# Hybrid decoder trunk on one core: the rotary stage's loads move to GpSimd's queue, the constants are made sooner, raw weights get a third buffer

## The chip, the core and the metric

The kernel runs on one core of a Trainium2 chip. The metric is the device time of one launch in microseconds (us), and lower is better. A core has TensorE (PE, matrix products), VectorE (DVE), ScalarE (ACT), GpSimd (POOL) and SyncE (SP). SP computes nothing here: it issues DMA transfers. ACT and POOL issue DMAs too, between their other instructions. Each engine works through its own list of instructions in order, so an instruction that waits holds up all that stand behind it on the same engine.

## What is computed

The reference is a two-layer decoder trunk on a sequence of 1024 tokens with 1024 channels. Each layer normalizes, projects once to 5376 columns, runs two token mixers side by side and merges them through gates:

```python
for layer in range(DEPTH):
    h = rms_norm(x, norm_w[layer])
    proj = h @ w_in[layer]
    (q, k, v, z_attn, q_h, f_h, i_h, g_h, gate_attn, gate_hgrn) = jnp.split(proj, split_points, axis=-1)
    q = partial_rope(q.reshape(B, T, N_HEADS, HEAD_DIM), positions)
    k = partial_rope(k.reshape(B, T, N_KV_HEADS, HEAD_DIM), positions)
    a = sliding_window_attention(q, k, v, attn_sinks[layer]) * jax.nn.silu(z_attn)
    ...
    b = o.reshape(B, T, HGRN_WIDTH) * jax.nn.silu(g_h)
    merged = (jax.nn.sigmoid(gate_attn) * (a @ w_up_attn[layer])
              + jax.nn.sigmoid(gate_hgrn) * (b @ w_up_hgrn[layer]))
    x = x + merged @ w_out[layer]
return rms_norm(x, final_norm_w)
```

`partial_rope` turns only the first 16 of each head's 64 channels: it multiplies by a cosine, and adds the partner channel (8 away) times a sine. Everything is float32.

## The kernel before

**Stages of a layer.** Normalize and transpose the activations, split every float32 number into a high and a low part (three matrix products then stand for one). Then 15 *pairs* (`pair`, L273): each takes two chunks of 128 columns of `w_in`, with a scheme that needs seven block products instead of eight; a block product is a group of 12 matmuls of 128x512. Where the first of the seven has been made ahead (`pair_first`, `gate_first`; the first 12 pairs of layer 0 and the first 11 of layer 1, L35), a pair is five groups, 60 matmuls, else seven. Then attention (L700 to L812), the recurrence (`core`, L866), the up-projections and the output projection.

**A pair's weights.** `load_chunk` (L85) loads a raw chunk of 512 KB into a tile with the tag `wraw` of the pool `wp`, which has two buffers (L48); SP issues it. A pair has two chunks, `wr` 0 and 1. DVE forms sums of their halves (L282, L283, L285, L286), ACT and DVE split those (L130, L131, L290, L291). The last reader of chunk 0 is L286 (where the first product was made ahead), of chunk 1 it is L291; only then is their buffer free for a later chunk.

**Results.** Two PSUM tiles `pb` and `pc` take a pair's groups in turn (three buffers, `pj`), DVE adds them out (L307), ACT applies scale or gate (`result`, L523) and stores to DRAM: `yd` for q, k and v, `gd` and `zd` for gates.

**Rotary.** `rotary` (L601) is a generator that the pairs from `TURN` = 9 on step forward once for each result (`use`, L641). It loads two tables, `cosT` and `sinT`, from DRAM (L604), and then for each of five tiles of q and k: the tile `y` (L610) and, with four small loads of 8 partitions each, the partner channels into the one tile `other` (L615), which stays in use from tile to tile. DVE multiplies by the tables and adds (L617, L619, L620), ACT and DVE split (L623, L625), and GpSimd stores the parts to `ksd` and `qsd` (L629 to L634), from where attention loads them (L689, L691). All loads of `rotary` are issued by SP.

**Constants.** `constants` (L393) is another generator, stepped once behind each pair (L646). Its last four steps make the tables: GpSimd clears a tile `tab` (L479), DVE fills it (L482 to L487), TensorE transposes it (L490), ACT copies and stores it (L492, L493).

**Memory.** Nearly all other big tiles are *slots* of 4 KB per partition in one pool of `NSLOT` = 40 that go round in turn, so a tile waits until the last reader of the tile that had its slot before is done.

**What sets the order.** The kernel is written as one sequence; a scheduler orders the instructions of each engine by what they need and when it expects that, and puts in the waits. The order that it makes is fixed when the kernel is built.

Of the kernel before, what the change touches and what calls it, by code (L numbers as in the profile page):

```python
# [10 lines left out]
F32 = mybir.dt.float32  # L11
# [6 lines left out]
P = 128  # L18
# [10 lines left out]
HALF = 8  # L29
IN_W = 5376  # L30
OQ, OKV, OZ, OQH, OF, OI, OG, OGA, OGH = 0, 512, 768, 1280, 1792, 2304, 2816, 3328, 4352
NLEV = 7
NSLOT = 40
NPAIR = 15
AHEAD = (12, 11)  # L35
TURN = 9
# [4 lines left out]
def trunk_kernel(ctx, tc, x, positions, norm_w, w_in, attn_sinks, hgrn_norm_w, w_up_attn,  # L41
                 w_up_hgrn, w_out, lb_logits, final_norm_w, c_ident, c_side, c_upper, c_diag, c_lev,
                 c_freq, out):
    nc = tc.nc
# [3 lines left out]
    wp = ctx.enter_context(tc.tile_pool(name="wp", bufs=2))  # L48
    sp = ctx.enter_context(tc.tile_pool(name="sp", bufs=NSLOT))
    ap_ = ctx.enter_context(tc.tile_pool(name="ap", bufs=2))  # L50
# [6 lines left out]
    def slot(shape, name, dt=F32):  # L57
        return sp.tile(shape, dt, tag="slot", name=name)
# [24 lines left out]
        return xn  # L83

    def load_chunk(w, c0, nm, k=KT, wide=False):  # L85
        raw = slot([P, k, P], f"wr_{nm}") if wide else wp.tile([P, k, P], F32, tag="wraw", name=f"wr_{nm}")
        nc.sync.dma_start(raw, w[:, c0:c0 + P].rearrange("(k p) c -> p k c", p=P))
        return raw

# [44 lines left out]
    def chunk(w, c0, nm, k=KT):  # L134

        return split_w(load_chunk(w, c0, nm, k), nm, [P, k, P])
# [238 lines left out]
    def split_rows(w, c0, n, nm, first=0):  # L375


        g = 1024 // n
        res = {}
        for k in range(0, KT, g):  # L380
            raw = wp.tile([P, g, n], F32, tag="wraw", name=f"wr_{nm}_{k}")
            nc.sync.dma_start(raw, w[k * P:(k + g) * P, c0:c0 + n].rearrange("(k p) c -> p k c", p=P))
            hi, lo = (split_w if k < first else split_slot)(raw, f"{nm}_{k}", [P, g, n])
            for j in range(g):
                res[k + j] = (hi[:, j], lo[:, j])
        return res


    tabs = [dp.tile([P, T], F32, name=f"tabs_{i}") for i in range(2)]
# [115 lines left out]
    consts = constants()  # L505


    for L in range(DEPTH):
# [5 lines left out]
        yd = [dp.tile([P, T], F32, name=f"yd_{L}_{j}") for j in range(6)]  # L514
# [8 lines left out]
        def result(m, c, r, o, src, own=None):  # L523

            n = src.shape[1]
            eng = nc.gpsimd if L == 0 and len(p1s) < 6 else nc.scalar
            d = own if own is not None else hp.tile([P, n], F32, tag="po", name=f"pq_{L}_{m}_{c}_{o}")
            if m < 3:
                S.activation(d, src, AF.Copy, scale=qkv[r][1])
                eng.dma_start(yd[r][:, o:o + n], d)  # L530
            elif m < 11 or c >= OG:
                S.activation(d, src, AF.Sigmoid if r < 2 * KT else AF.Silu)  # L532
                eng.dma_start(gd[r * P:(r + 1) * P, o:o + n], d)
            else:
                S.activation(d, src, AF.Silu)
                eng.dma_start(zd[:, r, o:o + n], d)
# [63 lines left out]

        def rotary():  # L601
            cosT, sinT = (slot([P, T], f"{n}T_{L}") for n in ("cos", "sin"))
            for t, d in zip((cosT, sinT), tabs):
                nc.sync.dma_start(t, d)  # L604

            o = slot([P, T], f"other_{L}")
            G.memset(o, 0.0)
            for n, j in enumerate((0, 1, 2, 4, 5)):
                y = slot([P, T], f"y_{L}_{j}")
                nc.sync.dma_start(y, yd[j])  # L610
                for r in range(2):
                    for i in range(2):
                        a = r * HD + i * HALF
                        b = r * HD + (1 - i) * HALF
                        nc.sync.dma_start(o[a:a + HALF], yd[j][b:b + HALF])  # L615
                yield
                V.tensor_tensor(out=y, in0=y, in1=cosT, op=ALU.mult)  # L617
                yield
                V.tensor_tensor(out=o, in0=o, in1=sinT, op=ALU.mult)  # L619
                V.tensor_tensor(out=y, in0=y, in1=o, op=ALU.add)  # L620
                yield
                hi = slot([P, T], f"yh_{L}_{j}", F32R)
                S.copy(hi, y)  # L623
                lo = y.bitcast(F32R)
                V.tensor_tensor(out=lo, in0=y, in1=hi.bitcast(F32), op=ALU.subtract)  # L625
                if n == 0:
                    for g, (own, far) in enumerate(((LO, HI), (HI, LO))):
                        for d, u in ((ksd[g][1 - g], (hi, lo)), (ksd[g][g], (lo, hi))):
                            nc.gpsimd.dma_start(d[own], u[0][own].bitcast(F32))  # L629
                            nc.gpsimd.dma_start(d[far], u[1][own].bitcast(F32))  # L630
                else:
                    for d, own, far in ((qsd[n - 1][0], LO, HI), (qsd[n - 1][1], HI, LO)):
                        nc.gpsimd.dma_start(d[own], hi[own].bitcast(F32))
                        nc.gpsimd.dma_start(d[far], lo[own].bitcast(F32))  # L634
                yield

        turning = rotary()
        for m in range(NPAIR):
            (c0, r0), (c1, r1) = pairs[m]

            def use(j, a, src, own):  # L641
                result(m, *pairs[m][j], a * 512, src, src if own else None)
                if m >= TURN:
                    next(turning, None)
            pair(wi, (c0, c1), parts, hT, f"{L}_{m}", p1s[m] if m < ahead else None, use)
            next(consts, None)  # L646
            if m == NPAIR - 2:
                vT, vn = slot([P, T], f"vT_{L}"), [slot([P, NB, P], f"vn_{L}")]
                nc.sync.dma_start(vT, yd[3])
# [35 lines left out]
        V.tensor_tensor(out=vd, in0=vn[0][:, 1:], in1=vn[0][:, :NB - 1], op=ALU.subtract)  # L685
        ks, qs = [], []
        wis = split_rows(wi, OI, 512, f"i{L}", 4)
        for g in range(2):
            ks.append([back(ksd[g][r], f"ks_{L}_{g}_{r}", nc.gpsimd) for r in range(2)])  # L689
# [125 lines left out]


        def up_load(w, m, nm):
            raw = wp.tile([P, 4, 2 * P], F32, tag="wraw", name=f"wr_{nm}")
            nc.sync.dma_start(raw, w[:, m * P:(m + 2) * P].rearrange("(k p) c -> p k c", p=P))
            return raw  # L820

        def up_chunk(w, m, nm):
            return split_w(up_load(w, m, nm), nm, [P, 4, 2 * P])
# [293 lines left out]

        wo = {}
        raws = [up_load(w_up_hgrn[L], 0, f"uh{L}_0")]
        for m in range(0, KT, 2):  # L1120
            w = split_w(raws.pop(0), f"uh{L}_{m}", [P, 4, 2 * P])
# [4 lines left out]
            for a in range(2):  # L1126
                u, t = u2s[m // 2][a]
# [19 lines left out]
        def split_a(a, nm):  # L1147
            return [split_slot(t, f"m{L}_{nm}_{i}", [P, 2, 512]) for i, t in enumerate(a)]
# [62 lines left out]
        m = split_a(a11, "s2")  # L1211
# [4 lines left out]
        m = split_a(a21, "s1")  # L1216
# [8 lines left out]
        m = split_a(a12, "s4")  # L1225
# [4 lines left out]
        m = split_a(a11, "s3")  # L1230
# [63 lines left out]
```

## Time and profile before

| what | value |
|---|---|
| time, median of 3 runs | 1426.08 us (1421.89 to 1428.80) |
| the profiled execution's own time | 1425.17 us |
| its span, from the first to the last instruction | 1423.4 us |
| mean granted TensorE clock | 0.992 |
| DVE busy, ACT busy, POOL busy | 70%, 49%, 6% of the span |
| mean DMA rate | 169 GB/s |

How to read the lines of the profile: in `wr<-in_w_in_dram` the tile that is written stands left of the arrow, what is read right of it, and L87 is line 87 of the kernel. A stretch of the table of stages has the busy time and the number of instructions of each engine, the granted clock of TensorE as a share of full speed, and the share of the DMA engines' time that was in use. In the chain of waits, each row is a start, a length and what the time went to. The profiled execution took 0.91 us less than the median.

### The profile page before, as it was taken

What the parts mean: (1) busy time and instruction counts of PE and PEld (TensorE: products, weight loads), DVE (VectorE), ACT (ScalarE), POOL (GpSimd) and SP (SyncE); (2) the same over time, 40 slices, a digit from 0 to 9 for tenths busy, and PEclk for the clock granted to TensorE, in tenths of its full rate; (3) what the DMA queues carried; (4) which work ended last, traced back from release to release, by engine and by line L of the source; (5) the groups of instructions that cost most, each with busy time, mean ns of one, the idle gap of its engine ahead of it and who ended that gap; (6) DMA issues with size and microseconds to landing.
All of it is one profiled execution on the core that took longest, in us unless ns stands there. A gap on an engine that the chain in (4) does not pass through costs nothing.

```text
span 1423.4 us, 21284 instructions
## 1 busy us (share of the span) xinstructions
PE 1389.6 (98%) x8108; PEld 1125.5 (79%) x8108; DVE 998.8 (70%) x1638; ACT 694.4 (49%) x1386; POOL 83.1 (6%) x141
## 2 busy tenths in 40 slices
PE   8999999999999999999999999989999999999997
PEld 7888777778777787888878788868887778788885
DVE  6867667752755779589976565776347378876998
ACT  8753424343884555313576332334448746443244
POOL 1100001120000001000010000010200000100000
PEclk9999999999999999999999999999999999999999
DMA  9433446787134652671255344576933366329303
GB/s 276 156 126 126 140 156 201 248 268 270 60 119 159 231 189 90 244 264 54 74 198 165 106 130 142 194 222 202 320 123 97 133 213 217 120 62 401 129 0 119
DMA packets 203639, 240.05 MB, mean 169 GB/s; under 512 B 13648, under 2 KB 140112, under 8 KB 203536
## 3 DMA queue, kind: packets, MB, share of 16 engines
q1 hardware_dynamic: 159184, 153.73, 32.8%
q10 hardware_dynamic: 34944, 52.44, 10.2%
q0 software_dynamic: 9408, 32.51, 7.2%
q8 instruction: 64, 1.05, 0.3%
q14 instruction: 39, 0.32, 0.1%
HBM read 160.00 MB, written 78.64 MB: 168 GB/s over the span
## 4 chain that ended last, share of the span: by engine, by line
PE 79%; DVE 8%; DMA 5%; ACT 4%; issue 2%; SPq 1%; ACTq 0%; DVEq 0%
PE pb L296 5%; PE pb L297 5%; PE pb L298 5%; DMA wr<-in_w_in_dram 4%; PE pc L296 3%; PE pc L297 3%; PE pc L298 3%; PE pg L265 2%; PE pg L267 2%; PE pg L266 2%; PE pj_qh L141 2%; PE pj_qh L142 2%; PE av L762 2%; PE pj_qh L143 2%; PE pi L789 2%; PE pi L788 2%
## 5 line engine op out<-in xcount | busy, mean ns | idle before, releaser
L130 ACT CAST whi_s<-ws 128x1024 fp32r<-128x1024 f32 x30 | 31.6, 1052 | 139.6 <-DVE ws L283 120.5
L130 ACT CAST whi_o<-wo 128x1024 fp32r<-128x1024 f32 x20 | 21.1, 1054 | 77.0 <-PE pu_uh L143 35.5
L282 DVE TENSOR_TENSOR ws<-wr 128x512 f32<-128x512 f32 x30 | 20.7, 690 | 52.7 <-DMA wr<-in_w_in_dram 52.7
L532 ACT ACTIVATE pq<-pq 128x512 f32<-128x512 f32 x60 | 37.8, 630 | 31.8 <-DVE pq L307 26.1
L296 PE MATMUL pb<-th,wl 128*128 128x512 f32 x120 | 48.6, 405 | 4.4 <-DVE pq L307 4.3
L141 PE MATMUL pu_ua<-wh_a,wlo_ua 128*128 128x512 f32 x128 | 52.4, 409 | 0.0
L307 DVE TENSOR_TENSOR pq<-pb,p 128x512 f32<-128x512 f32 x46 | 31.7, 689 | 29.2 <-PE pb L298 29.1
L296 PE MATMUL pb<-th,wlo_s 128*128 128x512 f32 x120 | 48.0, 400 | 3.5 <-DVE y L617 3.2
L265 PE MATMUL pg<-hh,wl_p 128*128 128x512 f32 (+1 forms) x128 | 47.8, 375 | 3.0 <-ACT p L269 2.9
L143 PE MATMUL pu_ua<-wh_a,whi_ua 128*128 128x512 f32 x128 | 50.5, 395 | 0.0
L142 PE MATMUL pu_ua<-wl_a,whi_ua 128*128 128x512 f32 x128 | 50.4, 394 | 0.0
L143 PE MATMUL pu_uh<-wh_b,whi_uh 128*128 128x512 f32 x128 | 49.8, 389 | 0.0
L141 PE MATMUL pu_uh<-wh_b,wlo_uh 128*128 128x512 f32 x128 | 49.8, 389 | 0.0
L142 PE MATMUL pu_uh<-wl_b,whi_uh 128*128 128x512 f32 x128 | 49.8, 389 | 0.0
L737 ACT ACTIVATE pr<-pr,mx 128x128 f32<-128x128 f32 x128 | 49.7, 393 | 0.0
L296 PE MATMUL pb<-th,wlo_t 128*128 128x512 f32 x120 | 47.3, 394 | 2.1 <-DVE wlo_t L131 2.1
L296 PE MATMUL pc<-hh,wlo_t 128*128 128x512 f32 x120 | 47.9, 400 | 0.1
L131 DVE TENSOR_TENSOR wlo_t<-ws,whi_t 128x1024 fp32r<-128x1024 f32 x30 | 36.7, 1223 | 15.9 <-ACT whi_t L130 15.9
L297 PE MATMUL pb<-tl,wh 128*128 128x512 f32 x120 | 47.7, 398 | 0.0
L298 PE MATMUL pb<-th,wh 128*128 128x512 f32 x120 | 47.7, 398 | 0.0
L297 PE MATMUL pb<-tl,whi_s 128*128 128x512 f32 x120 | 47.4, 395 | 0.0
L297 PE MATMUL pb<-tl,whi_t 128*128 128x512 f32 x120 | 47.4, 395 | 0.0
(419 smaller groups left out, 4419.1 us busy)
## 6 DMA issues: line engine op xcount, KB each, us to landing
wr<-in_w_in_dram SPq DMA_DIRECT2D x72, 512.0 KB
gd<-pq ACTq DMA_DIRECT2D x79, 256.0 KB
fq<-fq ACTq DMA_DIRECT2D x48, 256.0 KB
wr_p<-in_w_in_dram SPq DMA_DIRECT2D x23, 512.0 KB
x<-in_x_dram SPq DMA_DIRECT2D x16, 512.0 KB
qs<-qsd POOLq DMA_DIRECT2D x16, 512.0 KB, 8.1
u<-gd SPq DMA_DIRECT2D x16, 512.0 KB
ga<-gd SPq DMA_DIRECT2D x16, 512.0 KB
```

The lines of the kernel that those rows point to most:

```text
L130: S.copy(hi, raw)
L131: eng.tensor_tensor(out=lo, in0=raw, in1=hi.bitcast(F32), op=ALU.subtract)
L141: PE.matmul(acc, lhsT=ll, rhs=rh, start=i == 0, stop=False)
L142: PE.matmul(acc, lhsT=lh, rhs=rl, start=False, stop=False)
L143: PE.matmul(acc, lhsT=lh, rhs=rh, start=False, stop=i == n - 1)
L265: PE.matmul(acc, lhsT=wl[:, k], rhs=h[:, t], start=k == 0, stop=False, skip_group_check=q > 0)
L296: PE.matmul(acc, lhsT=wl[:, k], rhs=h, start=start and k == 0, stop=False, skip_group_check=not start)
L297: PE.matmul(acc, lhsT=wh[:, k], rhs=l, start=False, stop=False, skip_group_check=not start)
L298: PE.matmul(acc, lhsT=wh[:, k], rhs=h, start=False, stop=k == 3, skip_group_check=not start)
L307: V.tensor_tensor(out=out, in0=in0, in1=in1, op=ALU.add)
L532: S.activation(d, src, AF.Sigmoid if r < 2 * KT else AF.Silu)
L737: S.activation(pr[:, h], pr[:, h], AF.Exp, bias=mx[:, h:h + 1], accum_out=sm[:, h:h + 1])
```

## The change

- The loads of the tables, of `y` and of `other` are issued by GpSimd and no longer by SP.
- The loads for a tile come one step sooner: the first tile's with the tables, each later tile's right behind the sum of the tile before it.
- The generator of constants makes two steps behind each of the first two pairs, so its last table is made two pairs sooner.
- `wraw` has three buffers, in `load_chunk`, `split_rows` and `up_load`. The pool of slots has 39 instead of 40, which is the same 4 KB per partition.

```diff
-NSLOT = 40
+NSLOT = 39
...
-        raw = slot([P, k, P], f"wr_{nm}") if wide else wp.tile([P, k, P], F32, tag="wraw", name=f"wr_{nm}")
+        raw = slot([P, k, P], f"wr_{nm}") if wide else wp.tile([P, k, P], F32, tag="wraw", name=f"wr_{nm}", bufs=3)
...
-            raw = wp.tile([P, g, n], F32, tag="wraw", name=f"wr_{nm}_{k}")
+            raw = wp.tile([P, g, n], F32, tag="wraw", name=f"wr_{nm}_{k}", bufs=3)
...
         def rotary():
             cosT, sinT = (slot([P, T], f"{n}T_{L}") for n in ("cos", "sin"))
-            for t, d in zip((cosT, sinT), tabs):
-                nc.sync.dma_start(t, d)
 
             o = slot([P, T], f"other_{L}")
             G.memset(o, 0.0)
-            for n, j in enumerate((0, 1, 2, 4, 5)):
+
+            def load(j):
                 y = slot([P, T], f"y_{L}_{j}")
-                nc.sync.dma_start(y, yd[j])
+                nc.gpsimd.dma_start(y, yd[j])
                 for r in range(2):
                     for i in range(2):
                         a = r * HD + i * HALF
                         b = r * HD + (1 - i) * HALF
-                        nc.sync.dma_start(o[a:a + HALF], yd[j][b:b + HALF])
+                        nc.gpsimd.dma_start(o[a:a + HALF], yd[j][b:b + HALF])
+                return y
+
+            tiles = (0, 1, 2, 4, 5)
+            for t, d in zip((cosT, sinT), tabs):
+                nc.gpsimd.dma_start(t, d)
+            nxt = load(0)
+            for n, j in enumerate(tiles):
+                y = nxt
                 yield
                 V.tensor_tensor(out=y, in0=y, in1=cosT, op=ALU.mult)
                 yield
                 V.tensor_tensor(out=o, in0=o, in1=sinT, op=ALU.mult)
                 V.tensor_tensor(out=y, in0=y, in1=o, op=ALU.add)
+                if n < 4:
+                    nxt = load(tiles[n + 1])
                 yield
...
-            next(consts, None)
+            for _ in range(1 if m > 1 else 2):
+                next(consts, None)
...
-            raw = wp.tile([P, 4, 2 * P], F32, tag="wraw", name=f"wr_{nm}")
+            raw = wp.tile([P, 4, 2 * P], F32, tag="wraw", name=f"wr_{nm}", bufs=3)
```

The scheduler makes another order of it. In the names below, the first number is the layer and the next the pair (for `wr`, `ws`, `pq`) or the tile (for `y`, `yd`); the last is the program's own count. On SP, where the rotary stage of layer 0 begins, the order before has the loads of the tables and of the first tiles among the weights:

```order
L87 DMA wr_0_9_1_2054<-in_w_in_dram 128x8x128
L604 DMA cosT_0_2119<-tabs_0_136 128x1024
L87 DMA wr_0_10_0_2165<-in_w_in_dram 128x8x128
L87 DMA wr_0_10_1_2167<-in_w_in_dram 128x8x128
L604 DMA sinT_0_2120<-tabs_1_137 128x1024
L610 DMA y_0_0_2125<-yd_0_0_139 128x1024
L615 DMA other_0_2123<-yd_0_0_139 8x1024 x4
L87 DMA wr_0_11_0_2281<-in_w_in_dram 128x8x128
L87 DMA wr_0_11_1_2283<-in_w_in_dram 128x8x128
```

The changed kernel's SP has in the same place weights alone, up to the load of the v tile behind pair 14's first chunk:

```order
L87 DMA wr_0_9_1_2054<-in_w_in_dram 128x8x128
L87 DMA wr_0_10_0_2171<-in_w_in_dram 128x8x128
L87 DMA wr_0_10_1_2173<-in_w_in_dram 128x8x128
L87 DMA wr_0_11_0_2281<-in_w_in_dram 128x8x128
L87 DMA wr_0_11_1_2283<-in_w_in_dram 128x8x128
L87 DMA wr_0_12_0_2394<-in_w_in_dram 128x8x128
```

Everything of rotary has left SP. On GpSimd, behind the last table's clearing, the order before went straight to the stores of the first turned tile:

```order
L479 MEMSET tab_1_1_2038 128x512
L607 MEMSET other_0_2123 128x1024
L629 DMA ksd_0_0_1_161<-yh_0_0_2232 64x1024
L630 DMA ksd_0_0_1_161<-y_0_0_2125 64x1024
L629 DMA ksd_0_0_0_160<-y_0_0_2125 64x1024
```

The changed kernel's GpSimd has the loads of the tables and of two tiles between them:

```order
L479 MEMSET tab_1_1_1842 128x512
L605 MEMSET other_0_2121 128x1024
L619 DMA cosT_0_2119<-tabs_0_136 128x1024
L619 DMA sinT_0_2120<-tabs_1_137 128x1024
L609 DMA y_0_0_2125<-yd_0_0_139 128x1024
L614 DMA other_0_2121<-yd_0_0_139 8x1024 x4
L609 DMA y_0_1_2165<-yd_0_1_140 128x1024
L614 DMA other_0_2121<-yd_0_1_140 8x1024 x4
L638 DMA ksd_0_0_1_161<-yh_0_0_2238 64x1024
L639 DMA ksd_0_0_1_161<-y_0_0_2125 64x1024
```

So the load of the first `y` stands behind that of `sinT`, and the first tile's stores stand behind the second tile's loads. On DVE, the order before has the first tile's products among the work of pairs 9 and 10:

```order
L617 TENSOR_TENSOR y_0_0_2125<-y_0_0_2125,cosT_0_2119 128x1024
L307 TENSOR_TENSOR pq_0_9_12_2088<-pc_0_9_2075,pq_0_9_12_2088 128x512
L131 TENSOR_TENSOR wlo_0_10_t_2180<-ws_0_10_1_2170,whi_0_10_t_2179 128x1024
L307 TENSOR_TENSOR pq_0_9_21_2159<-pb_0_9_2074,p1_0_8_901 128x512
L291 TENSOR_TENSOR wl_0_10_2184<-wr_0_10_1_2167,wh_0_10_2183 128x512
L619 TENSOR_TENSOR other_0_2123<-other_0_2123,sinT_0_2120 128x1024
L307 TENSOR_TENSOR pq_0_10_12_2201<-pb_0_10_2187,p1_0_10_986 128x512
L620 TENSOR_TENSOR y_0_0_2125<-y_0_0_2125,other_0_2123 128x1024
```

In the changed kernel they stand at the end of pair 7 and in pair 8:

```order
L624 TENSOR_TENSOR y_0_0_2125<-y_0_0_2125,cosT_0_2119 128x1024
L307 TENSOR_TENSOR pq_0_7_21_1950<-pb_0_7_1878,p1_0_6_816 128x512
L291 TENSOR_TENSOR wl_0_8_1973<-wr_0_8_1_1956,wh_0_8_1972 128x512
L307 TENSOR_TENSOR pq_0_8_12_1990<-pb_0_8_1976,p1_0_8_901 128x512
L282 TENSOR_TENSOR ws_0_10_0_2175<-wr_0_10_1_2173 128x512
L307 TENSOR_TENSOR pq_0_8_22_2004<-pc_0_8_1977,p1_0_8_901 128x512
L131 TENSOR_TENSOR wlo_0_9_s_2061<-ws_0_9_0_2056,whi_0_9_s_2060 128x1024
L626 TENSOR_TENSOR other_0_2121<-other_0_2121,sinT_0_2120 128x1024
L307 TENSOR_TENSOR pq_0_8_22_2004<-pb_0_8_1976,pq_0_8_22_2004 128x512
L627 TENSOR_TENSOR y_0_0_2125<-y_0_0_2125,other_0_2121 128x1024
```

The rotary stage of layer 0 begins some two pairs sooner, and the sums of a weight chunk (`ws_0_10` in pair 8, where it was pair 9 before) are formed a pair further ahead.

## The prediction

> **What bounds the kernel now.** The page gives TensorE 1389.6 us of busy work in a span of 1423.4 us, so time can be had back only where TensorE stands still or runs slowly. I read the waits of TensorE first, then the table of stages around them, then the chain of waits that leads there. TensorE's waits between 225 and 310 us (layer 0), then between 900 and 1000 us (layer 1); the columns are total us, times, longest us:
>
> ```profile
> PE pb L296 <- DVE pq L307: 3.0, 1, 3.0
> PE pb L296 <- DVE wlo_a L131: 1.1, 1, 1.1
> PE pb L296 <- DVE wlo_s L131: 0.3, 1, 0.3
> ...
> PE pb L296 <- DVE y L617: 3.2, 1, 3.2
> PE pb L296 <- DVE wlo_t L131: 2.1, 1, 2.1
> ```
>
> TensorE is idle for 3.0 + 1.1 + 0.3 + 3.2 + 2.1 = 9.7 us, and both places are rotary stages. The table of stages shows that idle time is not all that is lost:
>
> ```profile
> core 0: us, PE busy (x) PEld busy (x) DVE busy (x) ACT busy (x) POOL busy (x), PEclk, DMA share, GB/s
> 104.00:118.00 14.00, 14.00 (x63) 11.45 (x62) 9.17 (x13) 4.53 (x6) 0.00 (x0) 1.00 0.40 130
> ...
> 245.00:272.00 27.00, 23.64 (x91) 18.65 (x90) 20.39 (x24) 10.99 (x14) 2.84 (x6) 0.87 0.82 246
> 272.00:299.00 27.00, 27.00 (x120) 22.06 (x119) 19.81 (x21) 12.30 (x18) 4.28 (x8) 1.00 0.78 245
> 299.00:326.00 27.00, 25.87 (x117) 20.94 (x116) 12.30 (x15) 10.57 (x16) 8.60 (x16) 1.00 0.87 308
> 930.00:957.00 27.00, 21.71 (x88) 17.21 (x87) 16.67 (x21) 11.65 (x14) 2.66 (x5) 0.94 0.85 237
> 957.00:984.00 27.00, 26.94 (x112) 21.66 (x111) 20.64 (x23) 9.90 (x14) 3.74 (x7) 0.94 0.71 203
> ```
>
> The second stretch of 27 us has full pace: 120 matmuls, 0.225 us each, which makes a pair of 60 matmuls 13.5 us. The others fall short of it by 29, 3, 32 and 8, together 72 matmuls or **16.2 us**. Of this 9.7 us is the idle time and the other 6.5 us the clock, granted at 0.87 and 0.94 in these stretches. In the plain pair stage (104 to 118 us: 63 matmuls in 14 us, where full pace makes 62) there is nothing to gain.
>
> The chain of waits says why. Rows in order of time (start us, us, what), from pairs before rotary, then layer 0, then layer 1:
>
> ```profile
> 147.27 0.67 DVE wl L291
> 147.96 4.51 DMA wr<-in_w_in_dram
> ...
> 249.21 0.69 DVE wl L291
> 249.92 10.67 DMA wr<-in_w_in_dram
> 260.64 0.48 issue
> 261.12 0.69 DVE pq L307
> 261.86 0.80 PE pb L296
> ...
> 289.81 9.21 DMA wr<-in_w_in_dram
> ...
> 926.83 12.31 DMA wr<-in_w_in_dram
> 939.16 0.69 DVE ws L282
> ...
> 945.75 8.56 DMA wr<-in_w_in_dram
> ```
>
> Each time, L291 frees the buffer of chunk 1, SP loads the next chunk 1 into it, and DVE waits for that. Alone the load takes 4.51 us, just in time. Beside rotary's traffic it takes 10.67, 9.21, 12.31 and 8.56 us, and the excess over 4.51 us (6.2, 4.7, 7.8, 4.1) stops DVE, whose in-order queue holds the additions (L307) that free TensorE's PSUM tiles.
>
> **The change part by part.** *Third buffer.* With three buffers in turn, a chunk 1 no longer waits for L291 of the chunk 1 before it but for L286, the last reader of the chunk 0 before it. DVE's instructions in order of time give the distance, in layer 0 and layer 1:
>
> ```profile
> 244.01 0.68 DVE L286 TENSOR_TENSOR ws<-wr,ws 128x512 f32<-128x512 f32 x1
> ...
> 249.21 0.68 DVE L291 TENSOR_TENSOR wl<-wr,wh 128x512 fp32r<-128x512 f32 x1
> ...
> 905.57 0.69 DVE L286 TENSOR_TENSOR ws<-wr,ws 128x512 f32<-128x512 f32 x1
> ...
> 911.53 0.68 DVE L291 TENSOR_TENSOR wl<-wr,wh 128x512 fp32r<-128x512 f32 x1
> ```
>
> The load starts 249.21 - 244.01 = 5.2 us sooner in layer 0 and 911.53 - 905.57 = 6.0 us in layer 1. Left of the four excesses: 6.2 - 5.2 = 1.0, nothing, 7.8 - 6.0 = 1.8, nothing. So of 16.2 us, 2.8 us may stay, and **13.4 us** go. I take no discount for the same bytes moving as before: SP's queue now holds weights alone, so no load of rotary can stand ahead of a chunk, and rotary begins two pairs sooner in layer 0 and one in layer 1, which spreads its bytes. What is late next, once the chunks are there, is TensorE itself.
>
> *Rotary's loads on GpSimd.* What an issue costs there, how long transfers take to land from there, and from SP:
>
> ```profile
> L634 POOL DMA_DIRECT2D qsd<-y x8 | 4.3, 544 | 6.0 <-DVE y L625 6.0
> ...
> yd<-pq POOLq DMA_DIRECT2D x6, 128.0 KB, 3.6
> ksd<-y POOLq DMA_DIRECT2D x8, 256.0 KB, 7.4
> ...
> DMA to landing us min/median/max: 2.9/6.3/9.9
> ```
>
> Rows: groups of GpSimd from 225 to 310 us (busy us, mean ns); median landings of GpSimd's DMAs; landings of `y` from SP. Two tables and five times five loads are 27 issues per layer, 27 x 0.544 = 14.7 us of GpSimd's time, which is idle otherwise. What could cost is DVE waiting for a landing, with L307 queued behind it and TensorE behind that. There are two such places.
>
> First, the first `y` of layer 0 stands on GpSimd behind `sinT`, which waits for the last table to be stored. From filling that table to issuing the load of `sinT`, and the lengths of DVE's rotary steps:
>
> ```profile
> 220.20 0.17 DVE L482 TENSOR_SCALAR tab<-sins 128x32 f32<-128x32 f32 x1
> ...
> 226.41 0.34 SPq L604 DMA_DIRECT2D sinT<-tabs  x1
> ...
> L617 DVE TENSOR_TENSOR y<-y,cosT 128x1024 f32<-128x1024 f32 x5 | 6.1, 1220 | 1.4 <-DMA y<-yd 1.4
> L619 DVE TENSOR_TENSOR other<-other,sinT 128x1024 f32<-128x1024 f32 x5 | 6.1, 1217 | 0.0
> L307 DVE TENSOR_TENSOR pq<-pb,p 128x512 f32<-128x512 f32 x5 | 3.4, 685 | 0.3 <-PE pb L298 0.3
> ```
>
> That is 6.2 us. The table is filled 0.7 us into pair 7, so `y` is issued at 0.7 + 6.2 + 2 x 0.54 = 8.0 us, and DVE wants it ahead of the pair's last addition, at 13.5 - 1.2 = 12.3 us. A landing in 4.3 us costs nothing; the median of 6.3 us makes DVE 2.0 us late, and the addition ends at 12.3 + 2.0 + 1.2 + 0.7 = 16.2 us, just when TensorE wants that PSUM tile (three buffers, 13.5 + 2.7 us). The longest, 9.9 us, would cost TensorE 3.6 us, once. I take 0, by the median.
>
> Second, the four short loads into `other` can start only behind the sum of the tile before. For the second tile that sum ends 36 matmuls into pair 8 plus L307 and the sum (8.1 + 0.7 + 1.2 = 10.0 us), and its product L626 stands behind the first addition of pair 9 and L624 (13.5 + 2.7 + 0.7 + 1.2 = 18.1 us): 8.1 us. Four issues take 2.2 us, which leaves 5.9 us to land, and 1.6 us more before TensorE waits (L626 and L307 end at 20.0 us, the PSUM tile is wanted at 13.5 + 8.1 = 21.6 us). Bounds for 32 KB: 3.6 us (nearest in size, from GpSimd) and 9.9 us. I take 3.6 us, hence 0; at 9.9 us TensorE loses 9.9 - 7.5 = 2.4 us a tile, for four tiles in each of two layers 19 us. A gain is not to be had here, since TensorE never waited for `other`. For small delays in between I enter **1.0 us**.
>
> *Constants and one slot less.* The same instructions stand two pairs sooner, beside pairs in which DVE has 9.17 of 14 us in use: nothing. One slot less makes each tile wait for the reader one place further on. Where it could show, in recurrence and output stages, stand these rows (stages; DVE's waits):
>
> ```profile
> 600.00:650.00 50.00, 50.00 (x222) 41.41 (x221) 43.83 (x46) 9.08 (x9) 0.00 (x0) 1.00 0.68 255
> ...
> DVE gs L914 <- DMA Q<-fq: 15.7, 3, 6.4
> ```
>
> TensorE is busy throughout there, so no gain, and DVE already waits for loads three times without stopping it. I take 0, with up to 2 us for a load that comes later.
>
> The sum for the profiled execution: 1425.17 - 13.4 + 1.0 = 1412.8 us. It lies 0.91 us under the median, so I forecast **1413.7 us**.
>
> **The rivals.** *The DMA engines, not the queue, are full.* Where the stalls lie they are in use at 0.82 to 0.87, and the bytes stay. If the chunks come later in step with their earlier start, half of the loss stays: 16.2 / 2 = 8.1 us back, 1.0 lost, 1419.0 us. Against it: in 272 to 299 us the engines are in use at 0.78 and TensorE has full pace.
>
> *DVE holds GpSimd's issues up.* If each issue had to wait for a DVE instruction with two inputs in SBUF (1.22 us), the four short loads would be ready 4.9 us later, 8.1 + 2.6 us after the sum instead of within 8.1 us (2.2 + 3.6 + 4.9 = 10.7 us); TensorE loses 2.6 - 1.6 = 1.0 us a tile, 8 us in all, and with the clock (16.2 us lost for 9.7 us idle) 13.4 us: about 1426 us, no change. Against it: the eight issues of `qsd<-y` took 544 ns in the mean, with DVE at 20.39 of 27 us in two-input work. The Trainium skill says in "Advanced Engine Details and Errata", GPSIMD Details, that GpSimd shares a read and a write interface with DVE and conflicts with DVE instructions that have two inputs in SBUF; by that rule this rival would hold, and the 544 ns do not bear it out. The Trainium skill's "SBUF — State Buffer", Who interferes with whom, narrows it to GpSimd instructions that read SBUF, and warns that two-port copies on DVE starve GpSimd's descriptors; this stage has hardly any such copy.
>
> *Slower: the short loads land late.* They go in a burst beside `y`, weights and stores. TensorE begins to lose at a landing of 7.5 us. At 9.9 us the 19 us of idle time with the clock (x 1.67) are 32 us: 1413.7 - 1.0 + 32 = 1445 us. It is slower than before once the loss exceeds 13.4 us, 1.0 us a tile, a landing of 8.5 us. For it: 7.4 us for `ksd<-y`. Against it: those are eight times 256 KB at once, and this is 32 KB, four times.
>
> **How the numbers follow.** Forecast 0.60 (1408 to 1418: all 16.2 us and a little more back, or 3.6 + 2 us of bounds lost); full DMA engines 0.18 (1417 to 1422); held issues 0.12 (about 1426); late landings 0.10. A measurement of this kernel can tell 0.5%, 7.1 us, from no change: faster is below 1419.0 us. Faster: 0.60 and half of the second, 0.69. Same: 0.09 + 0.12 = 0.21. Slower: 0.10. The first two cases and the good end of the third reach from 1408 to 1424 us.
>
> **What would show it.** Right: TensorE's waits in the two rotary stages shrink from 9.7 us to under 3 us, granted clock near 1.00 in all stretches of 27 us, weight loads still longer than 4.51 us on the transfer but gone from the chain. Wrong: DVE rows that wait for `y` or `other` for more than 2 us with TensorE idle behind them; or `wr` still in the chain with 8 us and more.

## The result and the profile after

The changed kernel takes 1433.58 us (median of 8 runs, 1431.70 to 1435.78), the kernel before 1424.91 us in the runs beside it (8, 1417.26 to 1428.80). The ratio is 1.0069, interval 1.0048 to 1.0090: **slower by 0.7%**, where 1413.7 us and faster was forecast. The profiled execution took 1435.35 us with a span of 1433.6 us, 10.2 us longer than before.

First, where along the program the 10.2 us came. The timeline of TensorE has the same instruction at the ends of the stages; in each row the start comes first. Before, then after: the end of layer 0's rotary stage (`pi`), the last of the products made ahead, 2.9 us before layer 1's first pair (`pg`), the end of layer 1's rotary stage (`pi`).

```profile
327.26 0.48 PE L788 MATMUL pi<-whi_i,hl 128*128 128x512 f32 x1
...
783.99 0.50 PE L265 MATMUL pg<-hh,wlo_p 128*128 128x512 f32 x1 [0.68 <-ACT p L269]
...
1024.97 0.48 PE L788 MATMUL pi<-whi_i,hl 128*128 128x512 f32 x1
```

```profile
327.94 0.48 PE L798 MATMUL pi<-whi_i,hl 128*128 128x512 f32 x1
...
788.14 0.50 PE L265 MATMUL pg<-hh,wlo_p 128*128 128x512 f32 x1 [0.68 <-ACT p L269]
...
1033.83 0.48 PE L798 MATMUL pi<-whi_i,hl 128*128 128x512 f32 x1
```

Layer 0's pairs end 0.7 us later. From there to `pg` it takes 460.2 us instead of 456.7 (+3.5), layer 1's pairs 245.7 instead of 241.0 (+4.7), and the rest to the end of the span 399.8 instead of 398.4 (+1.3). So 5.4 us were lost up to the ends of the rotary stages, where 13.4 were to be gained, and 4.8 us in stages that the change was to leave alone.

In the rotary stages TensorE waits longer than before, and at other places. Its waits in the changed kernel, from 200 to 310 us, then from 860 to 1010 us:

```profile
PE pb L296 <- DVE pq L307: 3.3, 2, 2.8
PE pc L296 <- DVE pq L307: 2.8, 3, 1.6
...
PE pb L296 <- ACT pq L321: 5.4, 2, 3.2
PE pc L296 <- DVE pq L307: 3.4, 3, 2.2
```

That is 14.9 us; the kernel before has 10.3 us in these two windows, of which the prediction shows 9.7. `L321` is a copy on ScalarE, but DVE stands ahead of it: from 951.65 us the chain of waits has L283 and L307 of DVE, then L532 and L321 (954.07 us) of ScalarE. The table of stages shows that the loss has also spread: three stretches of 27 us in and just ahead of the rotary stages, where full pace is 120 matmuls.

```profile
245.00:272.00 27.00, 23.73 (x96) 18.46 (x95) 18.00 (x23) 9.69 (x12) 4.72 (x9) 0.94 0.66 212
...
876.00:903.00 27.00, 23.79 (x104) 19.08 (x103) 14.87 (x21) 6.47 (x9) 3.64 (x7) 1.00 0.55 169
...
957.00:984.00 27.00, 23.76 (x93) 18.86 (x92) 19.17 (x22) 10.68 (x15) 8.89 (x17) 0.89 0.69 205
```

The third share from the right is the granted clock. The DMA engines are in use at 0.66, 0.55 and 0.69 of the time, less than in the two worst stretches before (0.82 and 0.85), and more is lost: 67 matmuls in the three, where those two lost 61. In the stretch from 876 us rotary has not begun its products yet, and the kernel before had full pace there.

The chain of waits shows the very link that the third buffer was to cut. Rows of the changed kernel, layer 0, then layer 1:

```profile
222.66 0.70 DVE wl L291
223.38 10.28 DMA wr<-in_w_in_dram
...
239.56 0.70 DVE wl L291
240.28 9.90 DMA wr<-in_w_in_dram
...
889.74 0.67 DVE wl L291
890.42 6.99 DMA wr<-in_w_in_dram
...
922.56 0.70 DVE wl L291
923.28 8.05 DMA wr<-in_w_in_dram
```

L291 still frees the buffer, and DVE still waits for the load behind it. Its waits for raw weights (from 180 to 310 us, from 800 to 1010 us), before and after:

```profile
DVE ws L282 <- DMA wr<-in_w_in_dram: 9.7, 4, 2.7
...
DVE ws L282 <- DMA wr<-in_w_in_dram: 31.1, 10, 5.6
```

```profile
DVE ws L282 <- DMA wr<-in_w_in_dram: 23.0, 7, 5.1
...
DVE ws L282 <- DMA wr<-in_w_in_dram: 42.8, 13, 5.8
```

From 40.8 to 65.8 us. Why that is so stands in the order of DVE's instructions around the first product of pair 7 (layer 0; the first row is the kernel before's L291, then an addition, then the wait):

```
225 L291 TENSOR_TENSOR wl_0_7_1847<-wr_0_7_1_1830,wh_0_7_1846 128x512
226 L307 TENSOR_TENSOR pq_0_7_12_1864<-pb_0_7_1850,p1_0_6_816 128x512
227 L282 TENSOR_TENSOR ws_0_8_0_1944<-wr_0_8_1_1942 128x512
228 L285 TENSOR_TENSOR ws_0_8_1_1945<-wr_0_8_0_1940,wr_0_8_1_1942 128x512
229 L307 TENSOR_TENSOR pq_0_7_22_1878<-pc_0_7_1851,p1_0_6_816 128x512
```

The changed kernel in the same place:

```
237 L291 TENSOR_TENSOR wl_0_7_1875<-wr_0_7_1_1858,wh_0_7_1874 128x512
238 L307 TENSOR_TENSOR pq_0_7_12_1892<-pb_0_7_1878,p1_0_6_816 128x512
239 L282 TENSOR_TENSOR ws_0_9_0_2056<-wr_0_9_1_2054 128x512
240 L285 TENSOR_TENSOR ws_0_9_1_2057<-wr_0_9_0_2052,wr_0_9_1_2054 128x512
241 L307 TENSOR_TENSOR pq_0_7_22_1906<-pc_0_7_1879,p1_0_6_816 128x512
```

The rows are the same but for one number: the L282 between the two additions is now that of pair 9, not of pair 8. In the changed kernel the load of `wr_0_9_1` waits for row 237, two rows above the instruction that needs it. The trace has the same: this L291 starts at 191.43 us, SP issues the load at 192.14 us, and the L282 starts at 196.72 us. The scheduler has spent the third buffer on doing the sums a pair sooner, and the distance from the release of a buffer to the wait for its load is one addition, as before.

### The profile page after: what moved, and what is told of

It is laid out like the page before. It is cut to its first block, busy times and chain, and to the rows that moved or that the text cites. A ratio compares the mean times of both kernels' runs of the same rounds, so it can differ in the third digit from the quotient of the medians.

```text
span 1433.6 us, 21278 instructions
## 1 busy us (share of the span) xinstructions
PE 1391.3 (97%) x8108; PEld 1123.6 (78%) x8108; DVE 996.8 (70%) x1638; ACT 694.6 (48%) x1386; POOL 111.2 (8%) x195
## 4 chain that ended last, share of the span: by engine, by line
PE 75%; DVE 9%; DMA 8%; ACT 5%; issue 2%; ACTq 0%; DVEq 0%; SPq 0%
DMA wr<-in_w_in_dram 6%; PE pb L296 4%; PE pb L298 4%; PE pb L297 4%; PE pc L296 2%; PE pc L298 2%; PE pc L297 2%; PE pj_qh L141 2%; PE pg L265 2%; PE av L772 2%; PE pj_qh L143 2%; PE pj_qh L142 2%; PE pi L799 2%; PE pg L267 2%; PE pi L798 2%
## 5 line engine op out<-in xcount | busy, mean ns | idle before, releaser
L532 ACT ACTIVATE pq<-pq 128x512 f32<-128x512 f32 x60 | 37.8, 631 | 106.9 <-DVE pq L307 105.9
L282 DVE TENSOR_TENSOR ws<-wr 128x512 f32<-128x512 f32 x30 | 20.8, 692 | 78.5 <-DMA wr<-in_w_in_dram 78.5
L296 PE MATMUL pb<-th,wlo_t 128*128 128x512 f32 x120 | 47.7, 398 | 3.7 <-DVE pq L307 3.5
L296 PE MATMUL pc<-th,wlo_s 128*128 128x512 f32 x120 | 47.2, 394 | 2.0 <-DVE pq L307 2.0
L298 PE MATMUL pb<-th,whi_s 128*128 128x512 f32 x120 | 48.1, 400 | 0.0
L131 DVE TENSOR_TENSOR wlo_t<-ws,whi_t 128x1024 fp32r<-128x1024 f32 x30 | 36.7, 1224 | 15.6 <-ACT whi_t L130 15.6
L298 PE MATMUL pb<-th,whi_t 128*128 128x512 f32 x120 | 47.5, 395 | 0.0
## 6 DMA issues: line engine op xcount, KB each, us to landing
u<-gd SPq DMA_DIRECT2D x16, 512.0 KB, 10.2
ga<-gd SPq DMA_DIRECT2D x16, 512.0 KB, 10.2
```

Of the source, the lines that this page charges most:

```text
L131: eng.tensor_tensor(out=lo, in0=raw, in1=hi.bitcast(F32), op=ALU.subtract)
L296: PE.matmul(acc, lhsT=wl[:, k], rhs=h, start=start and k == 0, stop=False, skip_group_check=not start)
L298: PE.matmul(acc, lhsT=wh[:, k], rhs=h, start=False, stop=k == 3, skip_group_check=not start)
```

## The experiments

Each kernel was timed beside the kernel before, which took 1422.2 to 1424.1 us there. "Distance" is the number of additions (L307) that stand on DVE between the last instruction for which SP waits before the load of a chunk 1 and the L282 that waits for that load: in plain pairs, then in pair 10 of layers 0 and 1, where the first tile is turned and its eight stores go out. "DVE" is its wait for raw weights, "PE" the idle time of TensorE before `pb` and `pc`, each from 180 to 310 and from 800 to 1010 us together (us).

| run | buffers, slots | queue | distance | DVE | PE | time, us | ratio (interval) |
|---|---|---|---|---|---|---|---|
| before | 2, 40 | SP | 1; 2, 2 | 40.8 | 10.9 | 1422 to 1425 | 1 |
| after | 3, 39 | GpSimd | 1; 1, 1 | 65.8 | 16.0 | 1433.58 | 1.0069 (1.0048 to 1.0090) |
| e1_third_alone | 3, 39 | SP | 1; 7, 3 | 34.9 | 8.1 | 1418.09 | 0.9967 (0.9951 to 0.9984) |
| e2_two_buffers | 2, 40 | GpSimd | 1; 1, 1 | 74.6 | 30.3 | 1447.89 | 1.0179 (1.0160 to 1.0197) |
| e3_after_on_sp | 3, 39 | SP | 1; 3, 3 | 42.4 | 9.0 | 1422.45 | 0.9996 (0.9985 to 1.0006) |
| e4_held_sums | 3, 39 | GpSimd | 4; 4, 4 | 7.3 | 1.6 | 1408.46 | 0.9900 (0.9882 to 0.9917) |
| e5_slots39 | 2, 39 | SP | 1; 2, 2 | 40.3 | 13.1 | 1430.65 | 1.0050 (1.0038 to 1.0063) |
| e6_two_buffers_sp | 2, 40 | SP | 1; 3, 3 | 47.7 | 16.3 | 1431.67 | 1.0060 (1.0046 to 1.0074) |
| e7_queue_alone | 2, 40 | GpSimd | 1; 2, 1 | 43.1 | 22.6 | 1449.42 | 1.0188 (1.0165 to 1.0211) |
| e8_third_held | 3, 39 | SP | 4; 7, 6 | 3.4 | 2.3 | 1408.42 | 0.9899 (0.9881 to 0.9916) |
| e9_held_less | 3, 39 | GpSimd | 2; 2, 2 | 25.7 | 6.2 | 1413.68 | 0.9931 (0.9912 to 0.9950) |
| e10_two_held | 2, 40 | SP | 2; 2, 3 | 6.0 | 5.6 | 1417.95 | 0.9960 (0.9944 to 0.9976) |
| e11_big_on_sp | 3, 39 | both | 1; 2, 2 | 56.1 | 17.5 | 1431.54 | 1.0055 (1.0034 to 1.0076) |
| e12_short_on_sp | 3, 39 | both | 1; 2, 2 | 48.9 | 15.4 | 1430.27 | 1.0039 (1.0023 to 1.0054) |
| e13_gp_held | 2, 40 | GpSimd | 2; 2, 2 | 12.2 | 5.2 | 1414.68 | 0.9945 (0.9926 to 0.9963) |
| e14_queue_held | 2, 40 | GpSimd | 2; 2, 2 | 11.2 | 17.2 | 1438.18 | 1.0107 (1.0088 to 1.0127) |
| e15_sp_held | 2, 40 | SP | 2; 3, 3 | 10.2 | 11.6 | 1423.28 | 0.9997 (0.9987 to 1.0008) |
| e16_slot_back | 3, 40 | SP | 4; 7, 6 | 6.1 | 4.7 | 1410.92 | 0.9913 (0.9896 to 0.9930) |
| e17_held_slot_back | 3, 40 | GpSimd | 4; 4, 4 | 7.9 | 3.6 | 1410.18 | 0.9905 (0.9889 to 0.9921) |
| e18_gp_held_more | 2, 40 | GpSimd | 3; 3, 3 | 0.4 | 6.2 | 1415.47 | 0.9944 (0.9928 to 0.9961) |

**The parts of the change.** e1 is the kernel before with `bufs=3` and 39 slots; e2 the changed kernel with two buffers and 40 slots; e3 the changed kernel with rotary's loads on SP:

```diff
-                nc.gpsimd.dma_start(y, yd[j])
+                nc.sync.dma_start(y, yd[j])
...
-                        nc.gpsimd.dma_start(o[a:a + HALF], yd[j][b:b + HALF])
+                        nc.sync.dma_start(o[a:a + HALF], yd[j][b:b + HALF])
...
-                nc.gpsimd.dma_start(t, d)
+                nc.sync.dma_start(t, d)
```

> Only the third buffer for raw weights and the 39 slots; rotary's loads and the constants stand as in the kernel before. Theory A (the lead is spent): on DVE the sum of a chunk 1 (L282) now stands a whole pair further ahead, again two places behind the L291 that frees the buffer of that very chunk, so the chain L291, load, L282 is as short as before: 1424 to 1434 us, TensorE still waits 8 us or more in the two rotary stages. Theory B (two queues share the DMA engines): what costs is rotary's loads on GpSimd's queue, beside the weight loads; without that the third buffer brings what the prediction said: 1411 to 1418 us.

> The changed kernel with two buffers for raw weights and 40 slots: rotary's loads on GpSimd's queue, ahead by a step, constants sooner. Theory A: the order of L282 is that of before, so no slower than before, 1416 to 1427 us. Theory B: the weight loads in plain pairs (4.5 us before) take 6 us and more where a table or a y is loaded beside them, and it is slower than before, 1430 to 1438 us.

> The changed kernel with all of rotary's loads issued by SP again (three buffers, the step ahead and the sooner constants stay). Theory A: L282 stays two places behind its L291, hence no better than the changed kernel, 1429 to 1438 us. Theory B: the loads stand behind the weights in one queue, so the weights are fast again: 1411 to 1420 us.

The third buffer alone is 4.1 us faster, a third of what was forecast, at the upper edge of theory B's range. The changed kernel without it is 25.7 us slower than before: so the move to GpSimd's queue, the step ahead and the sooner constants do harm, and the third buffer takes some of it back. With the loads on SP again nothing is lost and nothing gained. Theory B has the way that e1 and e2 go, but puts e2's loss 10 us too low, and e3 fits neither theory.

**The order of DVE.** e4 leaves everything of the changed kernel as it is and ties down one order: `issue_after` puts an instruction behind another in DVE's list, with no new wait. The anchor is the fourth of a pair's five additions.

```diff
-        V.tensor_tensor(out=s1, in0=a21, in1=a22, op=ALU.add)
+        behind = [tc.issue_after(added[-2].ins) if len(added) >= 2 else ExitStack() for _ in range(2)]
+        with behind[0]:
+            V.tensor_tensor(out=s1, in0=a21, in1=a22, op=ALU.add)
...
-        V.tensor_tensor(out=s3, in0=a11, in1=a21, op=ALU.subtract)
+        with behind[1]:
+            V.tensor_tensor(out=s3, in0=a11, in1=a21, op=ALU.subtract)
...
-        add(o12, C, o12)
+        added.append(add(o12, C, o12))
```

> The changed kernel with nothing but its order on DVE altered: the sums L282 and L285 of a pair may be issued only behind the fourth of the five additions of the pair two before it, some 8 us later than in the changed kernel, still more than a pair before TensorE needs them. Theory A: the loads get the time that the third buffer should have given, DVE's waits for raw weights in the two rotary stages fall below 15 us from 65.8 us, TensorE's below 4 us, 1411 to 1420 us. Theory B: the loads stay long and TensorE waits as before, 1428 to 1436 us.

1408.46 us, 25 us under the changed kernel and 2.5 us under theory A's range, with the same loads on the same queues. The weight loads are hardly shorter: from 150 to 330 us a median of 5.0 us, up to 12.8, where the changed kernel has 5.2, up to 10.3.

```profile
DMA to landing us min/median/max: 4.2/5.0/12.8
```

But DVE hardly waits for them any more (L282 is L286 in this kernel), and two of the three stretches above run at full clock and near full pace:

```profile
DVE ws L286 <- DMA wr<-in_w_in_dram: 4.3, 2, 2.9
...
DVE ws L286 <- DMA wr<-in_w_in_dram: 3.0, 1, 3.0
```

```profile
245.00:272.00 27.00, 25.62 (x112) 20.41 (x111) 25.11 (x30) 12.56 (x16) 8.60 (x17) 1.00 0.76 230
876.00:903.00 27.00, 27.00 (x120) 22.37 (x120) 18.00 (x25) 8.97 (x13) 1.55 (x3) 1.00 0.55 178
```

So what the third buffer could give was there, and the order gave it away. e9 holds the sums back by one addition only (the anchor is the second of the five), e8 holds them as e4 does in e1, with the loads on SP, and e10 holds them behind the second addition of the pair before in the kernel before, with two buffers:

> The changed kernel with the sums L282 and L285 held back by one addition only (behind the second of the five additions of the pair two before, where e4_held_sums has the fourth; in the changed kernel they stand behind the first). Theory A, with a dose: the load has one group of 12 matmuls more (2.7 us) where e4 gives it three, so part of the way from 1433 to 1408 us: 1414 to 1425 us. Rival (what helped in e4 was another order of the rest, not the time given to the load): within 3 us of 1433 or of 1408 us.

> Third buffer and 39 slots, the sums held back as in e4_held_sums, but rotary's loads and the constants as in the kernel before. Theory A (once the sums are held back the third buffer covers long loads too, so the queue no longer matters): 1405 to 1411 us, within 3 us of e4_held_sums. Theory Q alone (each long weight load costs, whatever the order on DVE): 1397 to 1403 us, clearly under e4_held_sums.

> The kernel before (two buffers, 40 slots, rotary on SP) with the same one addition between: L282 and L285 of a pair stand behind the second addition of the pair before it. With two buffers the sums are needed within the same pair, so holding them back takes from one side what it gives to the other. Theory A (it is the third buffer that makes room for holding back): 1418 to 1428 us, near the 1422 of the kernel before. Rival (the order alone does it, the third buffer is not needed): under 1414 us.

The dose works: distance 1, 2, 4 gives 1433.6, 1413.7, 1408.5 us (the middle one 0.3 us under theory A's range). Once the sums are held back by four additions, the queue makes no difference (e8 and e4, ratios 0.9899 and 0.9900). With two buffers the same means gives 6.0 us (e10), at the edge of theory A's range and less than half of what e4 and e8 have: order and buffer each have a share.

**The queue: transfers or order?** e6 is e2 with the loads on SP, e7 the kernel before with only the queue changed:

> Two buffers and 40 slots, the step ahead and the sooner constants, but all of rotary's loads issued by SP: differs from e2_two_buffers by the queue alone. Theory Q (what cost 25.7 us there is the queue: loads of another queue run beside the weight load that DVE waits for, loads of the same queue run behind it): 1420 to 1428 us. Theory S (what cost is that the step ahead and the sooner start put the loads where the weights and the stores are): 1438 us and more.

> The kernel before, with rotary's loads issued by GpSimd and nothing else: no step ahead, no sooner constants, two buffers, 40 slots. Theory Q: 1434 to 1450 us, weight loads of over 8 us in the chain where tables and tiles are loaded beside them. Theory S: 1420 to 1428 us.

The queue costs 16.2 us between e6 and e2, and 26.5 us by itself in e7; the step ahead and the sooner start cost 8.7 us in e6. e6 lies between the ranges of the two theories, e7 in theory Q's. That looked like theory Q, two queues that share the DMA engines. e11 and e12 move either the large loads or the short ones back to SP:

> The changed kernel with the tables and y (512 KB each) issued by SP again and only the short loads into other left on GpSimd. Theory Q1 (a large load of another queue shares the transfer with the weights): 1420 to 1426 us, like e3_after_on_sp. Theory Q2 (the queue costs because the short loads stand behind GpSimd's stores): 1431 to 1437 us, like the changed kernel.

> The reverse: tables and y on GpSimd as in the changed kernel, the short loads into other issued by SP. Theory Q1: 1431 to 1437 us, like the changed kernel. Theory Q2: 1420 to 1426 us.

Neither theory: e11 lies in Q2's range and e12 just under Q1's, and the two exclude each other. Against e3 each half on GpSimd costs 0.6% and 0.4%, more than half of what both cost together (0.7%). One load differs from the other sixteenfold in size, so shared bandwidth is a poor reason, though no run excludes it here; what both have in common is that the distance in pair 10 falls from 3 to 2. The next three tie the order down with two buffers, as e10 does:

> e2_two_buffers (two buffers, 40 slots, loads on GpSimd's queue, step ahead, sooner constants) with L282 and L285 held behind the second addition of the pair before, as in e10_two_held. Theory O (the queue costs by way of the order: with rotary's loads off SP the scheduler takes the weights to come sooner and puts L282 one addition behind the release of its load, where it puts it two or three behind with the loads on SP): most of the 25.7 us go, 1418 to 1430 us. Theory Q (the transfers of two queues share the DMA engines, whatever the order): 1438 to 1450 us.

> e7_queue_alone (only the queue changed) with the same holding back. Theory O: 1418 to 1432 us. Theory Q: 1438 to 1452 us. If it stays high with long waits for y or other instead of for the weights, neither holds, and what costs is that rotary's loads stand behind the stores in GpSimd's queue.

> e13_gp_held with rotary's loads on SP: under the same holding back the two differ by the queue alone. Theory O: within 5 us of e13_gp_held. Theory Q: 10 us and more under it.

e13 settles it for the changed kernel's arrangement: with all of rotary's loads on GpSimd's queue and the order tied, 33 us of e2 are gone, and it is no slower than the same with the loads on SP (e15), but 8.6 us faster. So theory Q, by which the transfers cost whatever the order, fails. Theory O holds in its direction (e13 is 3.3 us under its range); that the two come within 5 us it had wrong. Their orders still differ (distance 2 and 3 in pair 10), but the longer distance is that of the slower kernel, so this does not explain the 8.6 us, and their cause stays open. The longest weight load of the chain in layer 0, e2 first, then e13:

```profile
237.97 15.91 DMA wr<-in_w_in_dram
```

```profile
231.73 7.81 DMA wr<-in_w_in_dram
```

The load itself is shorter too, for the same transfers: in e2 GpSimd issues the first tile's stores from 234.39 to 239.61 us and this load begins among them, in e13 it begins ahead of all but one of them. The Trainium skill's "DMA: Bandwidth & Descriptors", Issuing engines are not separate DMA queues, says that transfers interleave on the same DMA engines whichever engine issued them, and that a further issuing engine saves no more than issue time. The pairs ahead of rotary's products in the changed kernel agree that they interleave (6.99 us instead of 4.51 beside a load of GpSimd). So a weight load beside the transfers of a second queue does take longer here; what e13 shows is that this costs little once the order leaves DVE something else to do in that time. How much of e2's loss is the longer load and how much the short distance, no run separates.

e14 is the third case of its expectation, in layer 0. It stays high: the tie takes only 11.2 of the 26.5 us away. DVE has no wait for weights there, but waits 9.6 us for `y`; without the step ahead, the loads of `y` and most of `other` stand on GpSimd behind the eight stores of the first tile. Rows of its chain:

```profile
243.88 5.78 DMA ksd<-yh
249.95 10.62 DMA other<-yd
```

This is the smaller part, though. Of the 15.7 us by which e14's profiled execution is longer than the kernel before's, 12.3 lie behind the two `pi`, in stages that the edit does not touch (in e7 it is 16.4 of 29.3). TensorE waits there for the next weights and for `hlo` (activations read back from DRAM), in one place 3.0 us for `hlo` alone. Why these loads come late in e7 and e14 was not followed up, so the 26.5 us of e7 are not explained by the distance on DVE.

**The slot.** e5 changes only `NSLOT`; e16 and e17 are e8 and e4 with 40 slots, where the 4 KB come from a tile for unused results:

```diff
-    junk = cp.tile([P, D], F32, name="junk")
+    def dump(n, nm):
+        return hp.tile([P, n], BF16, tag="po", name=f"junk_{nm}")
```

> The kernel before with 39 slots instead of 40 and nothing else. In the four runs with 39 slots so far the stages behind the rotary ones took some 3.5 us more than in those with 40. Theory A (one slot less costs later stages): 1424 to 1428 us, where the kernel before has 1422. Rival (those 3.5 us come from the third buffer's other uses): 1421 to 1423 us.

> e8_third_held with 40 slots: the 4 KB come from the tile that takes ScalarE's unused squares, which now go in bfloat16 into the rotating result tiles (the sums of squares are still taken in float32). If the slot is worth what e5_slots39 showed (7.7 us) or what the later stages of the changed kernel show (4.9 us): 1400 to 1405 us. Rival (what stalled there is covered, or the dumps delay the results): 1406 to 1411 us.

> e4_held_sums with the slot given back as in e16_slot_back (40 slots, the unused squares in bfloat16 into the rotating result tiles). In e16 the loss moved to layer 0's rotary stage, where DVE waited for the tile y on SP's queue; here y is loaded a step ahead by GpSimd, so if the slot is worth anything it shows: 1400 to 1405 us. Rival (one slot costs nothing once the sums are held back): 1406 to 1411 us.

> e13_gp_held (two buffers) with the sums held behind the third addition of the pair before instead of the second. If with two buffers the load and the time that the sums then have until TensorE wants the weights share one pair, the second addition is about the balance, and this one gains nothing: 1412 to 1422 us. Rival (the later the better, as from e9 to e4 with three buffers): 1405 to 1411 us, and the third buffer is not needed at all.

One slot less costs 7.7 us when nothing else is changed, more than theory A's range. Of these, 5.9 us show in e5's stages between and behind the pairs (from `pi` to the next layer's pairs 461.2 instead of 456.7 us, behind the second `pi` 399.8 instead of 398.4). Giving it back to a held kernel brings nothing: the rivals of e16 and e17 hold. Layer 0's pairs end 6.5 and 7.3 us later than in e8 and e4: 3.0 and 3.1 us are lost ahead of the first pair, and TensorE is idle for 4.3 and 3.6 us in one place behind it. The stages behind the two `pi` are only 0.7 and 1.8 us shorter. e13, with 40 slots, has late stages as long as e5's. So that the 4.8 us outside the rotary stages are the slot's price is not shown. e18 gains nothing over e13, as expected: with two buffers the sums must be early and late in the same pair.

## Why the prediction was wrong

*What bounds the kernel* was right for layer 1, where DVE waits 5.6 and 4.5 us for the two long loads. In layer 0 the chain was misread. The load of 10.67 us landed at 260.59 us, but DVE was then held by L131, and the L282 that needs the load started at 261.72 us without a wait. Rows of ScalarE and DVE before:

```profile
258.90 1.04 ACT L130 CAST whi_a<-wr 128x1024 fp32r<-128x1024 f32 x1 [5.05 <-PE pc L298]
```

```profile
259.98 1.22 DVE L131 TENSOR_TENSOR wlo_a<-wr,whi_a 128x1024 fp32r<-128x1024 f32 x1 [4.74 <-ACT whi_a L130]
261.12 0.68 DVE L307 TENSOR_TENSOR pq<-pb,pq 128x512 f32<-128x512 f32 x1
```

The addition that TensorE waited for stood behind the split of pair 12's chunk 0. ScalarE could begin that only when TensorE had read the tile that it writes; the load of chunk 0, issued at 244.72 us, landed at the same moment, 258.8 us. The load of chunk 1, which the third buffer was to bring forward, did not hold it. In the whole window from 180 to 310 us DVE waited 9.7 us for weights, at most 2.7 us at once, where the sum has excesses of 6.2 and 4.7 us.

That e4 and e8 got back 13.7 and 14.5 us, near the 13.4 us of the sum, is therefore partly luck. Their profiled executions gain 21.0 and 20.1 us up to the ends of the two rotary stages, more than the 16.2 us that the prediction saw to be had, and lose 4.4 and 3.4 us in the stages behind (the kernel before's profiled execution was 2 to 3 us longer than its medians beside them).

*The step that failed* is "with three buffers in turn, a chunk 1 no longer waits for L291 of the chunk 1 before it but for L286", and the 5.2 and 6.0 us from it. It took the buffers to go round in turn and DVE's order to stay. Neither held. Chunk 0 kept one buffer, and chunk 1 took the other two by turns, so it still waits for an L291, that of two pairs before: in pair 7, SP issues a chunk 1 at 192.14 us, when an L291 ends, and the next chunk 0 at 200.98 us, when an L286 ends. SP's waits in the changed kernel (190 to 310 us) show it:

```profile
SPq L87 <- DVE wl L291: 39.0, 5, 16.2
SPq L87 <- DVE ws L286: 32.8, 3, 12.4
```

And the sums that need the load moved a pair sooner with it. The row that says so, the L282 of pair 10 among the additions of pair 8, stands in the order quoted ahead of the prediction; it was seen as work done further ahead and given no price. A wait that is moved ahead in an in-order queue is a cost. So of the 13.4 us the buffer alone brought 4.1 (e1), and DVE's waits for weights rose from 40.8 to 65.8 us in the changed kernel.

*Rotary's loads on GpSimd* were costed by issue time and landing. Both estimates were near: in layer 1 the loads took 505 and 565 ns to issue.

```profile
L614 POOL DMA_DIRECT2D other<-yd x20 | 10.0, 505 | 24.6 <-DVE y L627 24.3 <-issue 0.3
...
L609 POOL DMA_DIRECT2D y<-yd x5 | 2.8, 565 | 32.8 <-DVE wlo_s L131 19.0 <-DVE wlo_t L131 13.8
```

DVE waited 0.7 us for `y` in one place and never for `other`, whose loads landed in time (in layer 1 with a median of 4.6 us). From DVE's waits and the DMAs of layer 0's stage (median us to landing last):

```profile
DVE y L624 <- DMA y<-yd: 0.7, 1, 0.7
```

```profile
y<-yd POOLq DMA_DIRECT2D x5, 512.0 KB, 5.5
...
other<-yd POOLq DMA_DIRECT2D x20, 32.0 KB, 3.3
```

The rule in "Advanced Engine Details and Errata", GPSIMD Details, of the Trainium skill, that GpSimd conflicts with DVE instructions with two inputs in SBUF, does not show in these issues, which took about as long as the 544 ns before.

What was missed is that with the loads off SP the order has L282 closer behind the release of its load: distance 3 with SP, 1 with GpSimd. That the scheduler takes the weights to come sooner is the likely reason; no run looks into it. Moving the loads costs 11 us with three buffers (e3 against the changed kernel) and 16.2 us with two (e6 against e2), and nothing where the order is tied (e4 against e8, e13 against e15).

*The reason against a discount* ("SP's queue now holds weights alone, so no load of rotary can stand ahead of a chunk") was half of it. In layer 1, ahead of rotary's products, the weights took 6.99 us (890.42, above) where a `y` was loaded beside them by GpSimd; alone they take 4.51. In the kernel before, SP issued both tables and the first `y` right behind such a load, and it was there by 903.05 us, 4.7 us after its issue. SP's timeline and DVE's:

```profile
898.38 0.37 SPq L87 DMA_DIRECT2D wr<-in_w_in_dram  x1
898.79 0.57 SPq L604 DMA_DIRECT2D cosT<-tabs  x1
```

```profile
903.05 0.69 DVE L282 TENSOR_TENSOR ws<-wr 128x512 f32<-128x512 f32 x1 [2.64 <-DMA wr<-in_w_in_dram]
```

*One slot less*, "0, with up to 2 us": the stages outside rotary lost 4.8 us, so the bound was too small, whatever the cause.

*The rivals.* Full DMA engines: no. In the changed kernel they are in use less than before, and e8 has full pace with them in use at 0.89:

```profile
921.00:948.00 27.00, 27.00 (x120) 22.16 (x120) 22.36 (x26) 12.94 (x17) 4.28 (x8) 1.00 0.89 259
```

Held issues: no, by the 505 and 565 ns. Late short loads: not in the changed kernel, but true of e7 and e14, which lack the step ahead. The rival that happened, an order of DVE in which the freed buffer buys nothing, was not among them.

## What to carry to other kernels

Where a scheduler sets the order, a buffer more or a queue relieved does not shorten a wait by itself: count, in the new order, what stands between the instruction that frees a buffer and the one that waits for its next load. If that distance is not longer, the lead has been spent. Tie the waiting instruction behind something later and measure again: here tying two sums of each pair turned 0.7% slower into 1.0% faster, and most of what looked like a cost of the queue went with it. It does not do everything: where the loads stood behind stores on their new queue (e14), less than half of the loss went.

## What the runs showed of the hardware

Idle time of TensorE costs more than itself: in e2 a wait of 10.8 us in layer 0 left 65 matmuls in 27 us and a granted clock of 0.81.

```profile
245.00:272.00 27.00, 16.16 (x65) 13.10 (x65) 15.28 (x21) 9.24 (x11) 4.73 (x9) 0.81 0.60 194
```

Full pace is 0.225 us a matmul, so 16.16 us of busy time would have held 72. And a load of 32 KB took 10.62 us (e14) when it was issued by the engine that had just issued eight stores of 256 KB and a load of 512 KB, against medians of 3.3 us (layer 0) and 4.6 us (layer 1) in the changed kernel, where it stands ahead of the stores.
